# Four small moves in a one-core encoder-block kernel: an early fold, a late transform, an earlier load and a longer slow start

## The chip, the cores and the metric

The kernel runs on one core of a Trainium2 chip. A core has a matrix engine (TensorE, PE in the profile), two elementwise engines (VectorE, DVE; GpSimd, POOL), an engine for functions of one input (ScalarE, ACT) and a queue that issues transfers (SyncE, SP). Each engine runs its own instructions strictly in the order in which the program lists them, and waits for the others through semaphores. The metric is the device time of one execution in microseconds (us). Lower is better.

## The reference

Two batches of 2048 rows by 1024 columns (called s = 0 and s = 1 below) go through the same layer with the same weights. For every batch:

```
u  = rmsnorm(h)
z  = u @ w_in                 # columns: q 512 | k 128 | v 128 | ga 512 | f 512 | gf 512
q, k = rope(rmsnorm per head) # 8 q heads, 2 kv heads, head size 64
a  = softmax(q k^T / 8) v  * silu(ga)
fo = Re(2-D DFT of f over (positions, 64 channels)), times a 64x64 map for each of 8 groups, * silu(gf)
h  = h + [a, fo] @ w_out
y  = rmsnorm(h + (p @ w_ple) * sigmoid(rmsnorm(h) @ w_ple_gate))
```

All of it is float32 in and out. The kernel splits float32 numbers into a high and a low float16 part, and forms a product as three float16 products (high by high, high by low, low by high).

## The kernel before, in words

**Two long stages.** The first stage (`project`, L607) makes u and all products with w_in, row by row. The second stage runs attention (`attention`, L1252) and weaves into it a second stream of work, the *fill*: the rest of the Fourier branch and the output products of the block. Both stages are one instruction order that the program writes out by hand; no planner moves instructions later.

**The first stage** treats the 32 tiles of 128 rows in 16 pairs, eight pairs for each batch. For a pair i there is:

- `sq_u`, `newton`, `hi_u`, `lo_u`: the row norm, u split into two float16 halves (`hl`), and a transposing transfer on SP's queue that makes `uc`, the operand that TensorE needs.
- `mm_tile`: the q and kv products of each of the two tiles, and their copies out of PSUM (`z`, `vs`). `norm_q`, `rope_q`, `hi_q`, `lo_q` make q and k from them, on GpSimd, VectorE and ScalarE.
- *The fold.* Pairs other than a batch's first hold rows t and 2048-t. Their sum and difference go through the f weights in one product in place of two. `fold_u` (L810, GpSimd) adds the halves of u, `fold_s` (L816, GpSimd) forms sum and difference, `fold_hl` (L822) splits them again: high part on ScalarE (L827), low part on VectorE (L828). The result is `uf`. It is done in two halves, h = 0 and 1, each for half of the inner dimension. The buffer of `fold_s` (tag `sq`, one buffer) is shared with the squares of `sq_u` and of q and k.
- *The sweep* of the pair (`sweep_chunk`): the f product (48 narrow matmuls, L1039), a copy `ft` by ScalarE (L1007), the gf product of tile 0, then `first()` (L1009): one float32 product of `ft` with a 128x128 DFT matrix (two at L1012 in the profile; for a batch's first pair ten shorter ones at L1016 and L1027), a copy `ge` by ScalarE and a store `gd` issued by GpSimd; then the gf product of tile 1, and four ga products.

The sweep of a pair runs one iteration after its `mm_tile`, and is cut into steps: 57 for an ordinary pair, 65 for a batch's first (a step of f or gf is estimated in the program at 0.64 us, one of ga at 0.32). `sweep_part(us)` (L793) issues steps until that many estimated microseconds are spent; between such calls the iteration places the other work, so that this order is the order on every engine. Every fifth step (`NBF = 5`) calls one step of a background list: `weights_far` (loads, scales and stores the weights of the second stage), `embed_rows` (the same for p) and last `channel_map` (L540), which loads the cosine table, the 64x64 maps and two masks, waits a number of background steps, makes two block products (L556) and stores them for the second stage. Another fifth step, from pair 14's iteration on, calls one step of `ahead`: four empty steps and then the row maxima of the first 14 attention steps (`maxima`, L1319), each two matmuls into two banks (L1330), and one step later two reductions by VectorE (L1338).

**Banks and slots.** The eight PSUM banks are given out by a counter: of eight in turn five are `ps_x`, two `ps_g`, one `ps_f` (L195). Within a kind, the bank that was released first is taken first. The outputs of ScalarE in the sweep and the tiles of the background list share ten SBUF slots (tag `w2k`).

**The prologue.** Pairs 0 to 4 are started by an order of their own, since weights arrive and have to be split first. The fold of pair 1 stands in it (diff below): half 0 ahead of the work on pair 3 (`sq_u(3)`, `mid`, `make_u(3, 0)`, which contains the newton steps and `norm_q(0)`), half 1 behind it.

**The second stage** has 64 units of 8 attention steps. After each step the program lets the fill run for a budget (`interleave`, L1802). The fill is taken as 756 us of TensorE work; a step has a share of it: 0 for every fourth step (which carries the product with v), otherwise 0.85 up to step `FIRST` = 30, 1 up to step 255 and 1.15 after it (L1459). What the fill has left when attention is done runs behind it alone.

Of the kernel before, what the change touches and what calls it, by code (L numbers as in the profile page):

```python
# [33 lines left out]
NBF = 5  # L34
# [1 line left out]
AH = 2  # L36
FP = 2
RATE = 1.15
FIRST, SLOW = 30, 0.85
LAG = 3  # L40
P32 = 7
WHOLE = 2 * NT - 2
# [123 lines left out]
class Build:  # L166
# [373 lines left out]
    def channel_map(self, pool):  # L540

        nc, a = self.nc, self.a
        tl = lambda n, *s: pool.tile(list(s), F32, name=n, tag="w2k", bufs=self.nw2k)
        m12, wf = tl("m12", 64, 4, 128), tl("wfm", 64, 8, 64)
        bd = [tl("bd", 128, 512) for _ in range(2)]
        nc.sync.dma_start(m12[:], a["c_m12"])
        nc.sync.dma_start(wf[:], a["w_fmix"].rearrange("o g c d -> c (o g) d"))
        for v in range(2):
            nc.sync.dma_start(bd[v][:], a["c_mask"][v])
        for _ in range(4):  # L550
            yield
        for v in range(2):
            ps = self.bank()
            cut = 256 if v else 384
            for i, sl in enumerate((slice(0, cut), slice(cut, 512))):
                nc.tensor.matmul(ps[:, sl], m12[:, 2 * v + i, :], wf[:].rearrange("c g d -> c (g d)")[:, sl],  # L556
                                 start=True, stop=True)
            nc.vector.tensor_tensor(out=bd[v][:], in0=ps[:], in1=bd[v][:], op=ALU.mult)
            yield
            nc.sync.dma_start(self.bdd[:, v], bd[v][:])  # L560
# [46 lines left out]
    def project(self, P, PU, W, early, later, wkv, wq, wf, wgf, wga, bg, mid):  # L607
# [25 lines left out]
        def load_x(i, tt):  # L633
                s, c = steps[i]
                x = PU.tile([128, DM], F32, name="x", bufs=5)
                nc.sync.dma_start(x[:], self.xrow(s, c * CH + tt))
                X.setdefault(i, []).append(x)

        def sq_u(i):
            SU[i] = st.tile([128, CH], F32, name="n_su", bufs=3)  # L640
            for tt in range(CH):
                j = P.tile([128, 2 * DM], F16, name="jk", tag="sq", bufs=1)
                nc.scalar.activation(j[:, :DM], X[i][tt][:], AF.Square, accum_out=SU[i][:, tt:tt + 1])
# [149 lines left out]
        def sweep_part(us):  # L793

            while us > 0 and sweeps:
                try:
                    us -= next(sweeps[0])
                    if done:
                        done.append(True)
                        if len(done) % NBF == 0:  # L800
                            next(bg, None)
                        if len(done) % NBF == 2:
                            next(self.ahead, None)
                except StopIteration:
                    del sweeps[0]

        sweeps, done = [], []
        UF, FT, FS = {}, {}, {}

        def fold_u(i, h):  # L810

            FT[h] = P.tile([128, CH, 512], F32, name="f_t", tag="t2", bufs=1)
            x = lambda b: U[i][:, :, b, 4 * h:4 * h + 4, :].rearrange("p t k r -> p t (k r)")
            nc.gpsimd.tensor_tensor(out=FT[h][:], in0=x(0), in1=x(1), op=ALU.add)

        def fold_s(i, h):  # L816
            x = FT.pop(h)
            FS[h] = P.tile([128, 2, 512], F32, name="f_s", tag="sq", bufs=1)
            for y, op in enumerate((ALU.add, ALU.subtract)):
                nc.gpsimd.tensor_tensor(out=FS[h][:, y], in0=x[:, 0], in1=x[:, 1], op=op)  # L820

        def fold_hl(i, h):  # L822
            if h == 0:
                UF[i] = P.tile([128, 2, 2, 8, 128], F16, name="uf", bufs=1)
            o = lambda b: UF[i][:, :, b, 4 * h:4 * h + 4, :].rearrange("p y k r -> p y (k r)")
            x = FS.pop(h)
            nc.scalar.activation(o(0), x[:], AF.Copy)  # L827
            nc.vector.tensor_tensor(out=o(1), in0=x[:], in1=o(0), op=ALU.subtract)  # L828
# [6 lines left out]
        def make_u(i, iq=None):  # L835

            sq = square_z(iq) if iq is not None else None
            rs = newton(iq, i, sq)
            hi_u(i)
            for tt in range(CH):  # L840
                lo_u(i, tt)
            if iq is not None:
                norm_q(iq, rs)
# [5 lines left out]
        def iteration(i):  # L849
# [21 lines left out]
            if ok(i):  # L871
                sweep_part(4.0)
                VL.pop((i, 0))()
                sweep_part(4.0)
            if ok(i - 1):
                norm_q(i - 1, rs)
            if folds(i):
                fold_u(i, 0)
                fold_s(i, 0)
                fold_u(i, 1)  # L880
                sweep_part(8.0)
                fold_hl(i, 0)
                fold_s(i, 1)
                sweep_part(7.0)
                fold_hl(i, 1)
# [86 lines left out]
        del stores_next[:]  # L972
        fold_u(1, 0)
        fold_s(1, 0)
        sweep_part(5.8)
        fold_hl(1, 0)
        sq_u(3)
        sweep_part(5.8)
        mid()
        make_u(3, 0)  # L980
        fold_u(1, 1)
        load_x(5, 1)
        sq_u(4)
        fold_s(1, 1)
        sweep_part(6.0)
        fold_hl(1, 1)
        sweep_part(1000.0)
        append(1)
        done.append(True)
# [7 lines left out]
    def sweep_f(self, s, c, uc, UF, i, pool, W):  # L997

        nc = self.nc
        CH = 2  # L1000
        w2k = lambda n, k=512: pool.tile([128, 512], F32, name=n, tag="w2k", bufs=self.nw2k)
        F = []
        half = (slice(0, EVEN), slice(EVEN, 512))

        def out(ps):
            F.append(w2k("ft"))
            nc.scalar.activation(F[-1][:], ps[:], AF.Copy, scale=self.sc["inv_f"][:])  # L1007

        def first():  # L1009
            pf = self.bank()  # L1010
            if c:
                nc.tensor.matmul(pf[:], self.dft1[:], F[0][:], start=True, stop=True)  # L1012
            else:
                for y, sl in enumerate(half):
                    for t in range(CH):
                        nc.tensor.matmul(pf[64 * t:64 * t + 64, sl], self.dft1x[:, 2 * t + y], F[t][:, sl],  # L1016
                                         start=True, stop=True)
            ge = w2k("ge")
            nc.scalar.activation(ge[:], pf[:], AF.Copy)
            if c:  # L1020
                nc.gpsimd.dma_start(self.gd[s][:, c, :], ge[:])
                return 0.86
            for t in range(CH):
                nc.gpsimd.dma_start(self.gd[s].rearrange("(g y i) t d -> y g i t d", g=8, y=2)[t, :, :, 0, :],
                                    ge[64 * t:64 * t + 64])
            px, gx = self.bank(), w2k("ge")
            nc.tensor.matmul(px[0:64, :EVEN], self.dft1x[:, 4], F[0][:, :EVEN], start=True, stop=True)  # L1027
            nc.scalar.activation(gx[0:64, :EVEN], px[0:64, :EVEN], AF.Copy)
            nc.gpsimd.dma_start(self.gxd[s], gx[0:64, :EVEN])
            return 1.3  # L1030

        if c:
            ps = self.bank()
            uf = UF.pop(i)
            n = 0
            for k in range(8):
                for ia, ib in SPLIT3:
                    for y, sl in enumerate(half):
                        nc.tensor.matmul(ps[:, sl], uf[:, y, ia, k, :], W["f"][:, ib, k, sl], start=n == y == 0,  # L1039
                                         stop=n == 23, skip_group_check=True)  # L1040
                    n += 1
                yield 0.64
            out(ps)
        else:
            for tt in range(CH):
                ps = self.bank()
                yield from self.mm(ps[:], lambda b, k: uc[:, tt, b, k, :], lambda b, k: W["f"][:, b, k, :])
                out(ps)
        for tt in range(CH):
            t = c * CH + tt  # L1050
            ps = self.bank()
            yield from self.mm(ps[:], lambda b, k: uc[:, tt, b, k, :], lambda b, k: W["gf"][:, b, k, :])
            gt = w2k("gt")
            self.silu2(gt[:], ps[:], self.sc["h_gf"], w2k("th"),
                       lambda t=t, gt=gt: nc.gpsimd.dma_start(self.gfd[s][t], gt[:]))
            if tt == 0:
                yield first()

    def sweep_ga(self, s, c, uc, pool, W):

# [958 lines left out]
```

## Time and profile before

| | us |
|---|---|
| runs | 2654.62, 2664.98, 2664.23; median 2664.23 |
| the profiled execution | 2668.79 |
| its span, first to last instruction | 2667.0 |
| TensorE busy in it | 2530.7 (95%) |
| GpSimd busy | 1885.7 (71%) |
| VectorE busy | 1695.7 (64%) |
| ScalarE busy | 1186.3 (44%) |
| mean granted TensorE clock | 0.984 of full speed |

The span has three parts: the first stage to about 800 us, the second stage with attention to about 2600, and the rest of the fill to 2667. A line of the timeline gives the start, the duration, the engine, the line of the program, the operation, output<-inputs, the shape, the count and, in brackets, how long the engine stood before it and what it waited for. Lines of several instructions (x24) give the time from the first start to the last end. Matmul ends are modelled, so the 24 matmuls of a product overlap by a little with the next ones.

### The profile page before, as it was taken

The page shows a single profiled execution, that of the slowest core. Times are in us where ns is not written, and L with a number is a line of the kernel's source. Part 1 is how long each engine was busy: PE and PEld are TensorE (multiplying, and loading weights), DVE is VectorE, ACT ScalarE, POOL GpSimd, SP SyncE. Part 2 cuts the span into 40 slices and gives each one's busy share as a digit, 9 for nine tenths or more (in the row PEclk, how much of TensorE's full clock was granted, in tenths as well). Part 3 has the DMA queues.
Part 4 walks back from the last instruction along what each step waited for, and adds up shares of the span by engine and source line. Part 5 has one row for each costly group of instructions (what it writes and reads, how often), then busy time and mean ns, then how long its engine had stood idle before and what let it go on. Part 6 is the DMA issues. An engine that isn't in the chain of part 4 may idle for free. (4 is left out here: it accounts for less than half of the span.)

```text
span 2667.0 us, 49778 instructions
## 1 busy us (share of the span) xinstructions
PE 2530.7 (95%) x19896; PEld 1376.4 (52%) x19896; DVE 1695.7 (64%) x2318; ACT 1186.3 (44%) x1983; POOL 1885.7 (71%) x1570
## 2 busy tenths in 40 slices
PE   6699999998989999999999999999999999999998
PEld 3366665665655644544445454544444445544543
DVE  7676576886566766655666666656555666666634
ACT  4433354433225534444544444544445445544442
POOL 0365545454548878877888888888888888888870
PEclk9899999998999999999999999999999999999999
DMA  8357588765548733222222223323222222222223
GB/s 252 100 159 201 152 236 218 190 171 133 142 120 258 230 117 78 50 74 60 62 66 68 68 72 97 84 69 77 76 62 68 71 75 72 75 77 72 70 59 83
DMA packets 450601, 297.92 MB, mean 112 GB/s; under 512 B 294000, under 2 KB 394736, under 8 KB 450368
## 3 DMA queue, kind: packets, MB, share of 16 engines
q1 hardware_dynamic: 438512, 257.00, 37.5%
q0 software_dynamic: 11856, 37.74, 3.9%
q8 instruction: 155, 2.54, 0.4%
q14 instruction: 78, 0.64, 0.1%
HBM read 146.12 MB, written 82.45 MB: 86 GB/s over the span
## 5 line engine op out<-in xcount | busy, mean ns | idle before, releaser
L1308 POOL TENSOR_TENSOR acc<-acc,p 128x1024 f32<-128x1024 f32 x384 | 925.5, 2410 | 142.6 <-ACT p L1303 106.8
L1338 DVE TENSOR_REDUCE a_mx<-ps_m 128x1 f32<-128x1024 f32 x498 | 608.9, 1223 | 559.6 <-PE ps_m L1330 548.5
L1303 ACT ACTIVATE p<-ps_s,s_scale 128x512 f32<-128x512 f32 x1024 | 648.0, 684 | 669.4 <-PE ps_s L1300 637.2
L1627 PE MATMUL ps_g<-w_pg,hT 64*128 64x512 f16 x2784 | 497.4, 377 | 0.5 <-DVE h L1553 0.5
L1366 PE MATMUL ps_o<-p,v 128*64 128x256 f32 x4096 | 468.5, 382 | 0.0
L1300 PE MATMUL ps_s<-q,k 64*128 64x512 f16 x3072 | 436.6, 378 | 15.1 <-ACT p L1303 14.8
L1366 PEld LDWEIGHTS ps_o<-p,v 128*64 128x64 f32 x4096 | 283.9, 137 | 160.1 <-issue 28.5
L491 PEld LDWEIGHTS <-uc 128*128 128x128 f16 x2400 | 237.5, 99 | 240.4 <-issue 32.4
L1627 PEld LDWEIGHTS <-hT 64*128 64x128 f16 x2784 | 204.6, 94 | 156.5 <-issue 11.6
L1627 PE MATMUL ps_g<-w_wo,mh 64*128 64x512 f16 x1440 | 261.9, 378 | 15.3 <-DVE mh L1537 14.0
L1300 PEld LDWEIGHTS <-k 64*128 64x128 f16 x3072 | 152.0, 94 | 216.3 <-issue 95.6
L1627 PE MATMUL ps_g<-w_wo,mT 64*128 64x512 f16 x1440 | 259.9, 379 | 0.5 <-DMA mT<-mh 0.5
L1330 PE MATMUL ps_m<-k,q 64*128 64x512 f16 x996 | 201.8, 377 | 13.9 <-DVE a_mx L1338 13.9
L1306 POOL TENSOR_TENSOR acc<-p,p 128x1024 f32<-128x1024 f32 x64 | 150.9, 2358 | 28.2 <-ACT p L1303 27.4
L491 PEld LDWEIGHTS <-w_ga 128*128 128x128 f16 x1536 | 150.2, 99 | 30.0 <-DVE w_ga L373 3.7
L1627 PEld LDWEIGHTS <-mh 64*128 64x128 f16 x1440 | 101.0, 94 | 107.1 <-DVE mh L1537 19.2
L1627 PEld LDWEIGHTS <-mT 64*128 64x128 f16 x1440 | 103.9, 95 | 83.4 <-issue 6.4
L754 POOL TENSOR_TENSOR t<-t,t 128x1280 f32<-128x1280 f32 x16 | 46.3, 2891 | 123.3 <-DVE t L750 123.3
L491 PE MATMUL ps_x<-w_gf,uc 128*128 128x512 f16 x552 | 129.2, 391 | 0.8 <-DVE w_gf L373 0.4
L1074 POOL DMA_DIRECT2D agd<-gat x64 | 35.1, 549 | 118.7 <-DVE gat L1084 113.7
L491 PE MATMUL ps_x<-uc,w_ga 128*128 128x256 f16 x1008 | 117.2, 277 | 0.0
L1389 DVE RECIPROCAL ps_f<-ps_f 128x256 f32<-128x256 f32 x61 | 107.1, 1756 | 9.1 <-PE ps_f L1382 9.1
(338 smaller groups left out, 3413.3 us busy)
## 6 DMA issues: line engine op xcount, KB each, us to landing
q<-qTd SPq DMA_DIRECT2D x256, 64.0 KB, 2.2
ag<-agd SPq DMA_DIRECT2D x64, 256.0 KB, 3.3
out<-h POOLq DMA_DIRECT2D x31, 512.0 KB, 3.0
x<-in_x_prompt SPq DMA_DIRECT2D x16, 512.0 KB, 5.0
gfd<-gt POOLq DMA_DIRECT2D x32, 256.0 KB, 2.7
w_st<-in_w_out SPq DMA_DIRECT2D x32, 256.0 KB, 3.9
agd<-gat POOLq DMA_DIRECT2D x64, 128.0 KB, 2.7
w_st<-in_w_ple_gate SPq DMA_DIRECT2D x32, 256.0 KB, 4.3
```

The costliest lines, as they stand in the source:

```text
L491: self.nc.tensor.matmul(ps, lhs(ia, k), rhs(ib, k), start=(i == 0), stop=(i == 3 * ks - 1))
L754: nc.gpsimd.tensor_tensor(out=t1[:], in0=t1[:], in1=t2[:], op=ALU.add)
L1074: nc.gpsimd.dma_start(self.agd[s][1, r * 128:(r + 1) * 128, c * n:(c + 1) * n], gt[:, :n])
L1300: nc.tensor.matmul(S[u][e][:], w[sl], q[sl].rearrange("p h q -> p (h q)"), start=j == i == 0, stop=i + 1 == len(todo), skip_group_check=True)
L1303: nc.scalar.activation(p[:, e, :], S[u][e][:], AF.Exp, scale=self.sc["s_scale"][:])
L1306: nc.gpsimd.tensor_tensor(out=ACC[u][:], in0=P[u, 0][:], in1=p[:], op=ALU.add)
L1308: nc.gpsimd.tensor_tensor(out=ACC[u][:], in0=ACC[u][:], in1=p[:], op=ALU.add)
L1330: nc.tensor.matmul(ps[c], Q[u][0][sl, h, :], kt[s, kv, half][sl, :, 0, :], start=True, stop=True)
L1338: nc.vector.reduce_max(MX[u][:, h, half, c:c + 1], x, axis=AX.X)
L1366: nc.tensor.matmul(o[64 * f:64 * f + 64], vt[s, kv, c // 8][:, c % 8, :], p[:, e, f], start=(c == 0), stop=(c == 15))
L1389: nc.vector.reciprocal(r, r)
L1627: nc.tensor.matmul(g[0][:], g[1](ia, k)[sl], g[2](ib, k)[sl], start=a, stop=z, skip_group_check=True)
```

## The change

Five edits in one diff.

1. Both halves of the fold of pair 1 are placed ahead of `sq_u(3)`; the estimated 5.8 us of sweep between half 0 and `mid` are split 3.0 + 2.8, and the 6.0 that stood between the parts of half 1 goes into what follows.
2. `first()` stands behind both gf products, in every sweep.
3. `channel_map` waits 8 background steps between its loads and its products, in place of 4.
4. `ahead` is called in every fourth sweep step, in place of every fifth.
5. The small share of fill (0.85) holds for attention steps 0 to 60, in place of 0 to 30.

```
-FIRST, SLOW = 30, 0.85
+FIRST, SLOW = 60, 0.85
...
-        for _ in range(4):
+        for _ in range(8):
             yield
...
                         if len(done) % NBF == 0:
                             next(bg, None)
-                        if len(done) % NBF == 2:
+                        if len(done) % (NBF - 1) == 2:
                             next(self.ahead, None)
...
         fold_u(1, 0)
         fold_s(1, 0)
+        fold_u(1, 1)
         sweep_part(5.8)
         fold_hl(1, 0)
+        fold_s(1, 1)
+        sweep_part(3.0)
+        fold_hl(1, 1)
         sq_u(3)
-        sweep_part(5.8)
+        sweep_part(2.8)
         mid()
         make_u(3, 0)
-        fold_u(1, 1)
         load_x(5, 1)
         sq_u(4)
-        fold_s(1, 1)
-        sweep_part(6.0)
-        fold_hl(1, 1)
         sweep_part(1000.0)
...
             self.silu2(gt[:], ps[:], self.sc["h_gf"], w2k("th"),
                        lambda t=t, gt=gt: nc.gpsimd.dma_start(self.gfd[s][t], gt[:]))
-            if tt == 0:
-                yield first()
+        yield first()
```

More of the change, by code (lines that the diff above doesn't have):

```diff
@@ L38 @@
 RATE = 1.15
-FIRST, SLOW = 30, 0.85
+FIRST, SLOW = 60, 0.85
 LAG = 3
@@ L549, in channel_map @@
             nc.sync.dma_start(bd[v][:], a["c_mask"][v])
-        for _ in range(4):
+        for _ in range(8):
             yield
@@ L801, in sweep_part @@
                             next(bg, None)
-                        if len(done) % NBF == 2:
+                        if len(done) % (NBF - 1) == 2:
                             next(self.ahead, None)
@@ L974, in project @@
         fold_s(1, 0)
+        fold_u(1, 1)
         sweep_part(5.8)
         fold_hl(1, 0)
+        fold_s(1, 1)
+        sweep_part(3.0)
+        fold_hl(1, 1)
         sq_u(3)
-        sweep_part(5.8)
+        sweep_part(2.8)
         mid()
         make_u(3, 0)
-        fold_u(1, 1)
         load_x(5, 1)
         sq_u(4)
-        fold_s(1, 1)
-        sweep_part(6.0)
-        fold_hl(1, 1)
         sweep_part(1000.0)
@@ L1055, in sweep_f @@
                        lambda t=t, gt=gt: nc.gpsimd.dma_start(self.gfd[s][t], gt[:]))
-            if tt == 0:
-                yield first()
+        yield first()
     def sweep_ga(self, s, c, uc, pool, W):
```

## Prediction

> **What bounds the kernel now.** I read the page first, then the waits of TensorE up to 900 us, then the timeline of each engine around each wait.
>
> ```profile
> PE 2530.7 (95%) x19896; PEld 1376.4 (52%) x19896; DVE 1695.7 (64%) x2318; ACT 1186.3 (44%) x1983; POOL 1885.7 (71%) x1570
> ```
>
> ```profile
> PE ps_g L1039 <- ACT uf L827: 16.4, 1, 16.4
> PE ps_x L556 <- DMA wfm<-in_w_fmix: 7.4, 1, 7.4
> PE ps_f L1012 <- ACT ft L1007: 7.3, 2, 5.8
> PE ps_x L1330 <- DVE a_mx L1338: 4.6, 1, 4.6
> PE ps_g L1012 <- ACT ft L1007: 3.4, 1, 3.4
> PE ps_x L1012 <- DVE a_mx L1338: 2.6, 1, 2.6
> PE ps_x L1012 <- ACT ft L1007: 1.9, 1, 1.9
> ```
>
> TensorE is busy 95% of the span, so time is won only where it stands. These rows (total, times, longest) are stalls in the first stage that the edits touch: 43.6 us together. A stall costs more than its length, because the clock is lower behind it:
>
> ```profile
> 392.70 5.34 PE L491 MATMUL ps_g<-w_gf,uc 128*128 128x512 f16 x24
> 403.81 2.07 PE L1012 MATMUL ps_f<-ft,dft 128*128 128x512 f32 x2 [5.76 <-ACT ft L1007]
> 405.68 7.14 PE L491 MATMUL ps_x<-w_gf,uc 128*128 128x512 f16 x24
> 543.58 2.08 PE L1012 MATMUL ps_g<-ft,dft 128*128 128x512 f32 x2 [3.37 <-ACT ft L1007]
> 545.45 7.22 PE L491 MATMUL ps_g<-w_gf,uc 128*128 128x512 f16 x24
> 138.72 1.02 PE L1012 MATMUL ps_f<-ft,dft 128*128 128x512 f32 x2
> ```
>
> The same 24 matmuls take 5.34 and 7.14 us, the same two 1.02 and 2.07. So the stall of 5.76 costs 5.76 + 1.05 + 1.80 = 8.6, that of 3.37 costs 3.37 + 1.06 + 1.88 = 6.3.
>
> *By the skill:* the Trainium skill, "TensorE: Matmul & The Clock Gate", section on the HAM clock gate, says that an idle window of about 3.4 us halves the clock until about 3.4 us of activity; by that a long stall costs 1.7 us extra, and my sum would be some 5 us smaller, 2631. The rows show 2.8 to 2.9, and a slow stretch after 2.58 us too (below), so the rows decide.
>
> **Edit 1, the fold.**
>
> ```profile
> 106.94 2.78 PE L491 MATMUL ps_x<-wr_kv,uc 128*128 128x256 f16 x24
> 128.72 1.03 PE L1039 MATMUL ps_g<-w_f,uf 128*128 128x264 f16 x4 [16.38 <-ACT uf L827]
> 144.76 1.47 PE L491 MATMUL ps_x<-uc,w_ga 128*128 128x256 f16 x12
> 97.61 2.49 POOL L820 TENSOR_TENSOR f_s<-f_t 128x512 f32<-128x512 f32 x2
> 122.91 2.11 POOL L814 TENSOR_TENSOR f_t<-uc 128x1024 f32<-128x1024 f16 x1
> 102.47 1.06 ACT L643 ACTIVATE jk<-x 128x1024 f16<-128x1024 f32 x1 [1.29 <-DVE uf L828]
> 115.22 2.19 ACT L681 ACTIVATE hl<-x,rsq_z 128x1024 f16<-128x1024 f32 x2 [8.68 <-DVE rsq_z L284]
> 101.22 1.23 DVE L828 TENSOR_TENSOR uf<-f_s,uf 128x1024 f16<-128x1024 f32 x1 [6.64 <-ACT uf L827]
> 110.85 1.48 DVE L655 TENSOR_REDUCE q_ss<-sq 128x20 f32<-128x1280 f32 x1
> 116.40 5.96 DVE L690 SCALAR_TENSOR_TENSOR hl<-x,rsq_z,hl 128x1024 f16<-128x1024 f32 x2 [0.81 <-ACT hl L681]
> 151.62 2.16 DVE L828 TENSOR_TENSOR uf<-f_s,uf 128x1024 f16<-128x1024 f32 x1 [5.26 <-ACT uf L827]
> 159.27 1.22 DVE L828 TENSOR_TENSOR uf<-f_s,uf 128x1024 f16<-128x1024 f32 x1
> ```
>
> The rows are of TensorE, GpSimd, ScalarE and VectorE. Half 1 is late because GpSimd does `norm_q(0)` first and comes to its `fold_u` at 122.9. New order on GpSimd: `fold_s` half 0 to 100.1, `fold_u` half 1 (2.1) to 102.2; the low split of half 0 on VectorE, beside it, I give the 2.16 of the row at 151.62 rather than its 1.23, so that it ends at 103.4, which frees the one buffer; `fold_s` half 1 to 105.9; high split (1.06) 107.0; low split (1.23) 108.2. The f product wants it at 109.6. **The 16.4 us wait goes.** Behind these on GpSimd stand the stores gfd, gd and gxd and the rope tables, which nobody awaits here.
>
> But what was moved past now comes later. `sq_u(3)` needs the shared buffer: 108.2 instead of 102.5, to 110.6 (two squares of 1.06 and their sums). Behind it on ScalarE stands the tanh of the second gf product, then on VectorE its product: two passes over 512 columns, which I put at 0.7 each, 112.0. Its bank is, by the counter and the order of release, the one that the kv product (106.94) takes, and in the new order `first()` no longer lies between. So **kv waits from 107 to about 112**, a new stall of 5 us; with a slow clock behind it f ends near 122 and the first gf product near 127. The second gf product takes the `ps_f` bank of the first ga product, whose reader on VectorE is queued behind newton and `lo_u(3)`: the setup constants and newton run 6 us later than before (q_ss at 116.8 for 110.85), `hi_u(3)` at 121.2 for 115.22, `lo_u(3)` (5.96) ends at 128.4, the reader at 128.8. From there 5.2 + 0.9 us (gf, `first()`) bring ga to 134.9; it was 144.76. Gain **10 us**. Bounds: 18.5 if neither bank holds it (16.4 and 2.1 of slow clock), 6 if VectorE's queue is 4 us later. Later folds don't gain with it, their slack covers it: `uf` of pair 2 was whole at 160.5 (last row) for a product at 170.8 (next fence), and is now just in time for one at 161. The transposes behind `lo_u(3)` land near 134 by the 5 us that two of them take on SP's queue; their q product stands near 153 (134.9 + 10.5 of ga + 7.8 of q and kv).
>
> **Edit 2, the transform.** Only its place moves: two matmuls, one copy, one store on GpSimd's queue, all behind the second gate's. TensorE then reads `ft` 10.4 us behind the f product, not 5.2. Is ScalarE merely late, or too slow?
>
> ```profile
> 401.68 0.28 ACT L720 ACTIVATE vs<-ps_x 128x128 f32<-128x128 f32 x1 [6.85 <-DMA vd<-vs]
> 339.86 2.18 ACT L681 ACTIVATE hl<-x,rsq_z 128x1024 f16<-128x1024 f32 x2
> 261.36 0.69 ACT L1007 ACTIVATE ft<-ps_x,inv_f 128x512 f32<-128x512 f32 x1 [4.80 <-PE ps_x L1039]
> 386.11 2.17 ACT L681 ACTIVATE hl<-x,rsq_z 128x1024 f16<-128x1024 f32 x2
> 170.84 5.40 PE L1039 MATMUL ps_x<-w_f,uf 128*128 128x264 f16 x48
> 213.38 5.40 PE L1039 MATMUL ps_g<-w_f,uf 128*128 128x264 f16 x48
> ```
>
> Here too slow: between 300 and 440, with the background weights, ScalarE needs 46.2 us for a pair, TensorE unstalled 42.5. In that stretch TensorE is freed once, by the 5.2 us of extra room, however many waits are named; about 4 us of the third wait return. The wait at 543 is an isolated one, and its lag (a gf product of 5.2 and 3.37) fits into 10.4: that 6.3 goes whole. Gain 5.2 + 6.3, **11 us**; bounds 5 and 18.4 (1.5 + 1.9 + 8.6 + 6.3). `ft` holds one of ten slots 5 us longer; I take that as nothing while ScalarE has idle time (44% busy), and price its failure as a rival. The copy `ge` and its store are read in the second stage only.
>
> **Edit 3, the channel map.**
>
> ```profile
> 651.38 2.04 PE L556 MATMUL ps_x<-wfm,m 64*128 64x384 f32 x4 [7.41 <-DMA wfm<-in_w_fmix]
> 653.36 3.38 PE L491 MATMUL ps_x<-uc,w_ga 128*128 128x256 f16 x15
> 658.67 4.35 PE L491 MATMUL ps_x<-uc,w_ga 128*128 128x256 f16 x24
> ```
>
> The loads stay, the products move by 20 sweep steps, across a q/kv block, some 30 us on: the transfer has landed. 24 such matmuls take 2.78 when warm, so 1.6 us of slow clock lie in the third row, as much in the second, and 1 each in the two block products: 7.4 + 5.3, **12.7 us**. The two VectorE products and stores fall in pair 13's f and gf, some 100 us ahead of their reader in the second stage. Four slots are held longer, when the background list is done with them. Bounds 9 (some of the slow stretch stays) and 12.7.
>
> **Edit 4, maxima sooner.** Counting steps: products at steps 710, 718, ... 814 rather than 717, 727, ... 847; the last pair's sweep begins at 808, so one of 14 falls into it instead of four.
>
> ```profile
> 773.61 1.15 PE L1012 MATMUL ps_x<-ft,dft 128*128 128x512 f32 x2 [2.58 <-DVE a_mx L1338]
> 774.55 3.78 PE L491 MATMUL ps_x<-w_gf,uc 128*128 128x512 f16 x9
> 782.97 1.18 PE L1330 MATMUL ps_x<-k,q 64*128 64x512 f16 x2 [4.63 <-DVE a_mx L1338]
> ```
>
> Both waits with their slow stretches cost 12: 2.6, 1.8 (9 matmuls in 3.78, 2.0 warm), 4.6, 0.8, and 2 behind the last row. Reductions 13 and 14 will sit where these two sit in VectorE's queue, behind newton and `lo_q`. By the order of release the second gf product then needs a bank of the one (from 770.5 to 773.5), the first ga product of the other (from 779.5 to 783.0): 6.5 us of waits stay, but none is queued behind them. More calls in pairs 13 and 14 meet a VectorE that waits there; the memset, the scaling of maxima and the transposed load `mr` move forward with them. Gain **5**; bounds 0 and 12.
>
> **Edit 5, the slow start.** 756 us over 420.85 shares are 1.8 us a share; steps 31 to 60 hold 22 with a share, so 22 x 0.15 x 1.8 = 6 us of fill leave a stretch near 910 to 1010 us (3.5 us a step from 801) and run behind attention.
>
> ```profile
> 925.00:950.00 25.00, 22.11 (x168) 13.44 (x164) 20.41 (x25) 15.06 (x26) 24.78 (x16) 1.00 0.56 165
> 2600.00:2667.00 67.00, 57.02 (x265) 25.64 (x262) 30.08 (x82) 14.13 (x21) 3.13 (x6) 0.96 0.35 84
> ```
>
> The columns are busy us of PE, PEld, DVE, ACT, POOL. TensorE is near its bound there and in the tail up to the last output, so the work only changes places: gain **0**; bounds a loss of 6 (GpSimd at 24.78 of 25 sets the step, nothing is saved) and a gain of 5 (less VectorE load takes its waits away).
>
> **Sum.** 10 + 11 + 12.7 + 5 + 0 = 38.7, against the profiled 2668.79 (span 2667.0): 2630. The median of the runs lies 4.6 below that execution, so **2626**. All low bounds: 14 won, 2650; all high ones 67, 2598.
>
> **The rivals.**
>
> *A, every stall goes* (18.5 + 18.4 + 12.7 + 12 = 61.6): 2603. For it: ScalarE is only 44% busy. Against: the two bank waits and the 46.2 us period. 0.14.
>
> *B, the lead is given back.* If the 46.2 us period between 300 and 440 is set by SP's queue regardless of when TensorE comes, the prologue's 10 us end in a longer wait there; left are 11 + 12.7 + 5, 2636, or 2641 with 6 from edit 2. Against: ScalarE waited for TensorE at 261 (its `ft`, 4.80), so it was level then and follows a TensorE that comes sooner. 0.17.
>
> *C, the change doesn't do what it says:* the waits of edits 1 and 2 return in full as bank waits, only edit 3 stays, edit 5 costs 6: 2657, no change. 0.10.
>
> *D, slower: slots.* `ft` and the map's tiles starve the ten slots; ScalarE then waits for stores (the 6.85 above is such a wait, on another buffer). From 3.5 us a pair over the 11 pairs with background work it eats the 39; at the 5.2 for which `ft` is held it is 57, and 2682. For it: a lag of 11 is already there (392.70 to 403.81). Against: stalls only bite once the lag passes 10.4. 0.06.
>
> **How the numbers follow.** The forecast has 0.53. Half a percent is 13 us, about what a measurement of this kernel tells from no change; faster means below 2651: 0.51 of the forecast's, all of A, 0.16 of B and 0.03 of C, 0.84. Same 0.11, slower 0.05. The range 2604 to 2653 holds nearly all between the forecast's bounds, and B; it leaves out half of A, most of C, and D, 0.2.
>
> **What would show it.** Right: no wait for `uf` near 112, a new one of some 5 us at the kv product near 107, ga of pair 1 near 135; waits for `ft` only near 400, below 5 us; none for `wfm`; one or two for a_mx near the end of the stage, 3 us each; attention some 39 us earlier than 800.8, and a tail 6 us longer. Wrong: attention less than 25 us earlier (B, C), ScalarE waits for slots in every pair (D), or a second stage that is longer by more than 6 us.

## The result and the profile after

The changed kernel takes 2619.08 us (median of 4 runs, 2618.91 to 2622.64) against 2664.61 (2654.62 to 2671.83) for the kernel before on the same chip: a ratio of **0.9835, 95% interval 0.9802 to 0.9868**. The forecast of 2626 lies 7 us above that and the range held it. The way to it was another than forecast, though: some 23 us were won ahead of attention, where 39 were forecast, and 22.8 behind it, where none were.

The profiled execution took 2622.64 us, its span is 2620.9. In the lines of the changed kernel all line numbers beyond some L1055 are one lower than before (L1338 is now L1337). The busy line of its page, then, from the list of what TensorE waited for from 0 to 800 us, the rows that bear on the edits (columns: total, times, longest):

```profile
PE 2519.7 (96%) x19896; PEld 1387.2 (53%) x19896; DVE 1704.0 (65%) x2318; ACT 1184.5 (45%) x1983; POOL 1875.5 (72%) x1570
```

```profile
PE ps_x L1329 <- DVE a_mx L1337: 7.9, 1, 7.9
PE ps_x L491 <- DVE a_mx L1337: 5.8, 2, 3.3
PE ps_g L1012 <- ACT ft L1007: 4.6, 1, 4.6
PE ps_x L1012 <- ACT ft L1007: 3.9, 1, 3.9
PE ps_x L491 <- DVE gt L1083: 3.8, 1, 3.8
PE ps_f L491 <- DVE gat L1083: 2.2, 1, 2.2
```

The waits for `uf` (16.4) and `wfm` (7.4) are gone. Two bank waits stand in the place of the first, as forecast; two `ft` waits stay where one was forecast; and the longest of these, 7.9, is a wait that the forecast did not have. The same things in TensorE's timeline of the changed kernel, and behind it three rows of the kernel before (the first q product, f of pair 13, attention's first matmul):

```profile
32.35 0.59 PE L491 MATMUL ps_x<-wr_q,uc 128*128 128x512 f16 x1 [7.62 <-ACT wr_q L372]
109.40 4.45 PE L491 MATMUL ps_x<-wr_kv,uc 128*128 128x256 f16 x24 [3.83 <-DVE gt L1083]
126.51 7.03 PE L491 MATMUL ps_f<-w_gf,uc 128*128 128x512 f16 x24 [2.24 <-DVE gat L1083]
134.23 2.02 PE L491 MATMUL ps_x<-uc,w_ga 128*128 128x256 f16 x17
160.31 5.40 PE L1039 MATMUL ps_x<-w_f,uf 128*128 128x264 f16 x48
392.64 1.97 PE L1012 MATMUL ps_x<-ft,dft 128*128 128x512 f32 x2 [3.87 <-ACT ft L1007]
532.65 2.03 PE L1012 MATMUL ps_g<-ft,dft 128*128 128x512 f32 x2 [4.63 <-ACT ft L1007]
646.45 4.75 PE L1039 MATMUL ps_f<-w_f,uf 128*128 128x264 f16 x42
655.54 1.13 PE L556 MATMUL ps_x<-wfm,m 64*128 64x256 f32 x4
674.02 0.58 PE L1329 MATMUL ps_x<-k,q 64*128 64x512 f16 x1 [7.87 <-DVE a_mx L1337]
756.14 5.34 PE L491 MATMUL ps_x<-w_gf,uc 128*128 128x512 f16 x24 [2.50 <-DVE a_mx L1337]
765.60 6.68 PE L491 MATMUL ps_x<-uc,w_ga 128*128 128x256 f16 x48 [3.27 <-DVE a_mx L1337]
777.68 0.81 PE L1299 MATMUL ps_s<-q,k 64*128 64x512 f16 x6
```

```profile
34.00 0.58 PE L491 MATMUL ps_x<-wr_q,uc 128*128 128x512 f16 x1 [7.69 <-ACT wr_q L372]
678.45 1.80 PE L1039 MATMUL ps_x<-w_f,uf 128*128 128x264 f16 x15
801.00 0.81 PE L1300 MATMUL ps_s<-q,k 64*128 64x512 f16 x6
```

Attention begins 23.3 us earlier. To see where, cut the first stage at three rows: the first q product of the prologue (32.35 after, 34.00 before: 1.65 us of the 23.3 are there ahead of the change), f of pair 2 (160.31 and 170.84) and f of pair 13 (646.45 and 678.45). The stretches took 128.0 us against 136.8, 486.1 against 507.6, and 131.2 against 122.5. So 30.3 us were won, and **8.7 lost again** in the last stretch. Of both, 2.1 us are work that crossed a mark: the two block products of the channel map (1.06 us each at full clock) stand ahead of f of pair 13 in the kernel before (651.38 and 656.67) and behind its start in the changed one (651.13 and 655.54). Without them 28.2 us were won and 6.6 lost.

Why TensorE stood 7.87 us at 674 is on the other engines. The changed kernel's timelines of SP's queue, GpSimd and VectorE:

```profile
644.12 3.07 SPq L1269 DMA_DIRECT2D k<-kTd  x4
654.14 1.06 SPq L1275 DMA_DIRECT2D v<-vd  x2
655.24 0.43 SPq L625 DMA_DIRECT2D rt<-in_c_rope  x1
```

```profile
658.84 0.72 POOL L630 TENSOR_TENSOR rt<-rt,g_q_t 128x256 f32<-128x256 f32 x1 [8.78 <-DMA rt<-in_c_rope]
673.12 0.13 POOL L1333 MEMSET a_mx<- 128x16 f32 x1
```

```profile
673.28 1.29 DVE L1337 TENSOR_REDUCE a_mx<-ps_x 128x1 f32<-128x512 f32 x2 [8.16 <-POOL a_mx L1333]
```

VectorE's first reduction for the products made ahead waits for a memset of 0.13 us on GpSimd. That memset stands behind a norm and folds, the norm behind the small load `rt`, and SP issued `rt` only after 16 loads of k and q and two of v (644 to 655). The products, now ahead of time, meet a GpSimd that is late.

The second stage: what TensorE waited for from 800 us on, before and then after. (`p` is ScalarE's exponential of the scores; `mh` is the split input of the fill's output product, whose low half VectorE writes; `seen` is a copy of one column by which a bank is let go.)

```profile
PE ps_s L1300 <- ACT p L1303: 16.8, 42, 1.7
PE ps_g L1627 <- DVE mh L1537: 14.0, 10, 3.2
PE ps_m L1330 <- DVE a_mx L1338: 13.9, 18, 2.6
```

```profile
PE ps_m L1329 <- DVE a_mx L1337: 14.4, 20, 2.6
PE ps_g L1626 <- DVE seen L1592: 6.5, 2, 5.3
PE ps_s L1299 <- ACT p L1302: 3.6, 9, 0.9
PE ps_g L1626 <- DVE mh L1536: 1.7, 2, 1.0
```

And busy times from attention's first matmul to ScalarE's last `p`, then from there to the end, before and then after. The columns are the window and its length, busy us (and instructions) of PE, PEld, DVE, ACT and POOL, the granted clock, the share of the DMA engines and GB/s:

```profile
801.00:2580.00 1779.00, 1727.75 (x14810) 877.03 (x14808) 1098.98 (x1057) 862.36 (x1428) 1495.31 (x1205) 1.00 0.32 86
2580.00:2667.00 87.00, 77.02 (x396) 34.66 (x392) 36.16 (x89) 20.01 (x31) 15.21 (x30) 0.97 0.30 72
```

```profile
778.00:2513.00 1735.00, 1706.99 (x14748) 883.48 (x14744) 1096.97 (x1052) 862.17 (x1427) 1483.44 (x1205) 1.00 0.33 88
2513.00:2621.00 108.00, 92.54 (x458) 39.41 (x453) 43.97 (x95) 20.58 (x31) 17.69 (x30) 0.88 0.27 70
```

Attention is 44 us shorter: TensorE idles 28 us in it instead of 51, and is busy 20.8 us less, with 62 matmuls moved behind it. The rest of the fill is 21 us longer, with 15.5 more of busy time (at a lower clock) and 5.5 more of idle time. Net, 23 us.

### The profile page after: what moved, and what is told of

Same layout as the page of the kernel before. It is cut to its first block, busy times and chain, and to the rows that moved or that the text cites. A ratio compares the mean times of both kernels' runs of the same rounds, so it can differ in the third digit from the quotient of the medians.

```text
span 2620.9 us, 49788 instructions
## 1 busy us (share of the span) xinstructions
PE 2519.7 (96%) x19896; PEld 1387.2 (53%) x19896; DVE 1704.0 (65%) x2318; ACT 1184.5 (45%) x1983; POOL 1875.5 (72%) x1570
## 5 line engine op out<-in xcount | busy, mean ns | idle before, releaser
L1337 DVE TENSOR_REDUCE a_mx<-ps_m 128x1 f32<-128x1024 f32 x498 | 608.9, 1223 | 513.1 <-PE ps_m L1329 502.0
L491 PEld LDWEIGHTS <-w_ga 128*128 128x128 f16 x1536 | 152.0, 100 | 49.1 <-issue 22.8
L491 PE MATMUL ps_x<-w_gf,uc 128*128 128x512 f16 x480 | 106.0, 379 | 2.5 <-DVE a_mx L1337 2.5
## 6 DMA issues: line engine op xcount, KB each, us to landing
agd<-gat POOLq DMA_DIRECT2D x64, 128.0 KB, 2.8
```

The source lines that it names most:

```text
L491: self.nc.tensor.matmul(ps, lhs(ia, k), rhs(ib, k), start=(i == 0), stop=(i == 3 * ks - 1))
L1337: nc.vector.reduce_max(MX[u][:, h, half, c:c + 1], x, axis=AX.X)
```

## The experiments

All times stand against the kernel before, measured beside each; it had medians of 2661.4 to 2664.9 in all of them. The three stretches are those above. Equal code differs in them from run to run: over all runs of this section, 126.3 to 129.1 us in the first, 485.2 to 488.4 in the second, and in the last 128.2 to 131.6 in the five whose order there is the changed kernel's. In the rows "before" and "map 4 steps" the 2.1 us of the map's products belong to the second stretch, in the others to the last. Of the parts undone alone, only the slow start differs from the changed kernel beyond the intervals of the whole times; the prices of the others rest on the stretches.

| kernel | q to f(2) | f(2) to f(13) | f(13) to attention | time, us | ratio to before, 95% |
|---|---|---|---|---|---|
| before | 136.8 | 507.6 | 122.5 | 2664.61 | |
| after | 128.0 | 486.1 | 131.2 | 2619.08 | 0.9802 to 0.9868 |
| after, old fold | 136.9 | 485.2 | 131.2 | 2630.77 | 0.9861 to 0.9891 |
| after, old place of f's transform | 129.7 | 489.7 | 124.3 | 2622.96 | 0.983 to 0.9863 |
| after, map 4 steps | 128.4 | 500.8 | 123.2 | 2628.66 | 0.9848 to 0.9904 |
| after, ahead every 5th | 126.6 | 485.3 | 127.7 | 2616.75 | 0.9808 to 0.984 |
| after, memset on VectorE | 129.1 | 485.8 | 122.4 | 2614.35 | 0.98 to 0.9833 |
| the same, ahead every 5th | 126.4 | 485.6 | 127.2 | 2614.52 | 0.9808 to 0.984 |

### The longer slow start, undone alone and done alone

In the changed kernel:

```
-FIRST, SLOW = 60, 0.85
+FIRST, SLOW = 30, 0.85
```

and in the kernel before:

```
-FIRST, SLOW = 30, 0.85
+FIRST, SLOW = 60, 0.85
```

> The changed kernel with the small share of fill for 30 steps again (the last part of the change undone alone). Attention's first matmul stands at 777 us either way. Theory S, the longer small share is what made the stretch from attention's first matmul to the end 22.8 us shorter (1866.2 before, 1843.5 after): the stretch is 1866 again and the time some 2641 us. Rival T, that stretch is shorter because attention starts from another state (earlier, with other work left over), whatever the share: the stretch stays at 1843 and the time at 2619. In between if both share in it.

> The kernel before with the small share for 60 steps, nothing else changed. Attention starts at 801 us as before. Theory S: the stretch behind it falls from 1866 to about 1843, time 2642 us. Rival T: no change, 2664 us; and below 2664 by 6 at most if only the fill that moves counts.

Measured: 2642.87 us (0.9906 to 0.9938) and 2636.05 us (0.9889 to 0.9921). From attention's first matmul to the end it is 1866.0 us in the first (777.3 to 2643.3) and 1843.2 in the second (797.8 to 2641.0). Theory S holds: the last part of the change, alone, takes 22.8 us off that stretch, from whichever start (1866.0 before, 1843.2 after). The runs below that differ from the changed kernel only ahead of attention took 1839 to 1845 us there, so the difference is well clear of the spread. In the changed kernel with 30 steps, TensorE's waits for `p` and `mh` behind 800 us are near those of the kernel before again:

```profile
PE ps_s L1299 <- ACT p L1302: 15.7, 39, 1.7
PE ps_g L1626 <- DVE mh L1536: 9.7, 8, 2.4
```

### How much is held back, or when

Two kernels, one with

```
-FIRST, SLOW = 60, 0.85
+FIRST, SLOW = 30, 0.70
```

and one with

```
-FIRST, SLOW = 60, 0.85
+FIRST, SLOW = 90, 0.85
```

> The changed kernel with the slow start shortened to 30 steps again but at share 0.70 instead of 0.85: by step 60 the same share of fill is held back (22 x 0.30 = 6.6 against 44 x 0.15 = 6.6), only sooner. Theory P, what counts is how far the fill stands behind attention afterwards (its place against attention's units): the time stays at 2619 us, with p and mh waits of some 4 and 2 us behind 800 us. Theory Q, what counts is the lighter load in steps 31 to 60 themselves: the time goes back to 2641 us, with p and mh waits of some 16 and 10 us.

> The changed kernel with the small share for 90 steps, so 3.3 shares (6 us of fill) more held back. If the gain grows with what is held back: another 10 to 24 us less, 2595 to 2610 us. If 60 steps already took nearly all of the p and mh waits (5.3 us are left) and the rest only swells the work behind attention: 2614 to 2625 us. If it is a matter of where the fill's tiles happen to fall against attention's units: some of the waits come back, 2625 to 2645 us.

Measured: 2624.5 us (0.9838 to 0.9868) and 2628.17 us (0.985 to 0.9884). The third, run last, has the memset of the next experiment as well:

```
-                    nc.gpsimd.memset(MX[u][:], -3e38)
+                    nc.vector.memset(MX[u][:], -3e38)
-FIRST, SLOW = 60, 0.85
+FIRST, SLOW = 45, 0.85
```

> The changed kernel with the memset on VectorE and the small share for 45 steps, half way between 30 and 60. So far, from attention's first matmul to the last p and from there to the end of the span: 1778.5 and 87.5 us with 30 steps, 1735.4 and 108 with 60, 1731 and 113 with 90. If both follow what is held back evenly: 1757 and 98 us, with attention's start at 771 a time of 2626 us, worse than the 2614 of 60 steps. If the waits for p and mh go at some point short of 45 and the rest only swells the tail: 1735 to 1743 and 95 to 101 us, a time of 2603 to 2613 us, better than both kernels.

Measured: 2620.86 us (0.9834 to 0.9867). Side by side, from attention's first matmul to the start of the last row of `p`, and from there to the end, of each kernel. Held back: the steps up to and with number `FIRST` that carry a share, 24, 35, 46 or 69 by the program's rule, times 1 less the share; the expectations counted a little fewer.

| slow start | shares held back | attention | rest | both |
|---|---|---|---|---|
| 30 steps at 0.85 | 3.6 | 1779 | 87 | 1866 |
| 45 at 0.85 | 5.3 | 1760 | 90 | 1851 |
| 60 at 0.85 | 6.9 | 1735 | 108 | 1843 |
| 30 at 0.70 | 7.2 | 1743 | 102 | 1845 |
| 90 at 0.85 | 10.4 | 1731 | 113 | 1844 |

Theory P holds in its main point: about the same amount held back sooner gives the same stretch within the spread, so the load of steps 31 to 60 is not what matters. (Of its waits, mh came to 0.9 us and p to 7.1, more than the 4 expected.) In the profiles the gain grows with the amount to some 7 shares and stops there: at 10.4 attention loses another 4 us, and the rest gains 5. The whole times say less for 90 steps: the profiled execution (2622.61) was the fastest of its four, and the median of 2628.17 lies in the range expected if waits come back. In that profile they did not: `p` has 3.8 us, `mh` none, and new are 3.4 us for `acc_h` and 2.4 more for `h`. Whether 90 steps are worse than 60 stays open, since the intervals overlap. The expectation for 45 steps, "both follow evenly" at 1757 and 98, is nearer than its rival, though the rest grew by only 3. What it is in attention that a later fill spares, wait by wait, no run took apart.

### The memset

```
-                    nc.gpsimd.memset(MX[u][:], -3e38)
+                    nc.vector.memset(MX[u][:], -3e38)
```

> The changed kernel with one edit: the memset that prepares a_mx for the products made ahead is issued on VectorE instead of GpSimd. Theory: the 7.87 us wait at 674 us is the first reduction's wait for that memset, which stands in GpSimd's order behind a norm that waits for a late load; the memset on VectorE takes it away, attention starts 11 to 14 us earlier (763 to 766 us) and the time is 2605 to 2608 us. Rival, VectorE itself is late there or the products meet another wait at the same place: the stall stays at 5 us or more and the time at 2617 to 2620 us.

Measured: 2614.35 us (0.98 to 0.9833). The wait of 7.87 us is gone; the longest at these products is now 1.89 us, at a later one of them:

```profile
676.95 0.37 PE L1329 MATMUL ps_x<-k,q 64*128 64x512 f16 x1 [1.89 <-DVE a_mx L1337]
```

The last stretch falls from 131.2 to 122.4 us, 8.8 where 11 to 14 was expected, and attention starts at 771.2, not by 766 (the run was 1.6 us later at the first q product). The cause is shown; the price was set too high. It is known only roughly: the last stretch took 128.2 to 131.6 us in five runs with the memset on GpSimd and 122.1 to 122.4 in three with it on VectorE, which is 5.8 to 9.5 us. In whole times the gain over the changed kernel, 4.7 us between medians taken on different occasions, is within their intervals.

### The ahead products, with the stall and without

```
-                        if len(done) % (NBF - 1) == 2:
+                        if len(done) % NBF == 2:
```

> The changed kernel with the ahead products asked for at every 5th step again. Theory: the 7.87 us wait for a_mx at 674 us and the slow clock behind it (some 11 to 14 us together) go, and the waits near the end of the first stage come back at their size of before (6 us more): attention starts at about 770 us and the time is 2609 to 2614 us. Rival, the part is worth the 5 us that the forecast gave it and the stall at 674 us comes with any spacing: attention starts at 783 us, time 2624 us.

> The changed kernel with the memset on VectorE and the ahead products at every 5th step again. It measures the fourth part alone, free of the stall at 674 us, against the kernel with the memset on VectorE and every 4th step (attention's first matmul 122.4 us after f of pair 13 begins). The forecast's price: 5 us dearer, 127 us. Rival, the part is worth nothing because the waits near the end of the stage only change places: 122 to 123 us. In time 2609 to 2619 us.

Measured: 2616.75 us (0.9808 to 0.984) and, with the memset moved, 2614.52 us (0.9808 to 0.984). With the memset on VectorE, every 4th step against every 5th is 122.4 against 127.2 us in the last stretch: the part alone is worth **4.8 us** there, against the 5 of the forecast; the whole times of the two, 2614.35 and 2614.52, do not tell them apart. One of the waits of the kernel before stands there again, longer than its 4.63:

```profile
753.09 0.58 PE L1329 MATMUL ps_x<-k,q 64*128 64x512 f16 x1 [6.38 <-DVE a_mx L1337]
```

With the memset on GpSimd it is 128.2 to 131.6 against 127.7: the stall is the price of sooner products and eats up at least what they win. The stall at 674 does not come "with any spacing", but the theory's 770 us for attention's start was missed too (772.6), and so was its time of 2609 to 2614.

### The fold

The hunk of the prologue goes back: half 1 of the fold behind `make_u(3, 0)`, as in the kernel before.

> The changed kernel with the second pair's folds back in their old order (first part of the change undone alone). Theory: the wait of 16.4 us for uf comes back in place of those of 3.8 and 2.2 us, and the lead that it costs stays lost: attention's first matmul at 786 to 788 us instead of 777.7 and the time 2627 to 2630 us. Rival, the period of 46.2 us between 300 and 440 us takes the lead back whenever it was won: attention starts at 777 to 780 us with smaller ft waits, time 2619 to 2622 us.

Measured: 2630.77 us (0.9861 to 0.9891), attention at 786.99. The wait is back, and of the lead that it costs nothing returns later (the other stretches are equal within 1 us):

```profile
128.44 1.03 PE L1039 MATMUL ps_g<-w_f,uf 128*128 128x264 f16 x4 [16.46 <-ACT uf L827]
```

### f's transform

```
+            if tt == 0:
+                yield first()
-        yield first()
```

> The changed kernel with f's transform behind the first gate product again (second part undone alone). Theory: the ft waits at 393 and 533 us grow to the 5.8 and 3.4 us of before and one more returns, with slow clocks 7 us in all by the traces (the forecast said 11): attention's first matmul at 784 to 789 us, time 2626 to 2631 us. Rival, once the prologue runs ahead ScalarE has caught up and the place of the transform no longer matters: 777 to 779 us, time 2619 us.

Measured: 2622.96 us (0.983 to 0.9863), attention at 778.71. Neither was quite right. With the fold placed early TensorE comes sooner, and the waits for `ft` are more than in the kernel before (9.88 in the prologue is new):

```profile
131.02 2.07 PE L1012 MATMUL ps_f<-ft,dft 128*128 128x512 f32 x2 [9.88 <-ACT ft L1007]
534.05 2.08 PE L1012 MATMUL ps_g<-ft,dft 128*128 128x512 f32 x2 [3.56 <-ACT ft L1007]
679.93 0.37 PE L1330 MATMUL ps_x<-k,q 64*128 64x512 f16 x1 [3.10 <-DVE a_mx L1338]
```

By f of pair 13, 5.3 us are lost (1.7 and 3.6); the 1.7 lie within the spread of equal code there, the 3.6 little beyond it. Then the last row: a TensorE that comes later waits 3.10 us at the late memset and not 7.87, and 6.9 us return. From the first q product to attention the kernel without the part is even 1.6 us shorter (743.7 against 745.3), and the intervals of the whole times overlap: what the part is worth in the changed kernel as a whole is not shown. Ahead of that stall a lead is partly lost whatever won it.

### The channel map

```
-        for _ in range(8):
+        for _ in range(4):
             yield
```

> The changed kernel with the channel map's products after 4 steps of the background list again (third part undone alone). Theory: TensorE then asks for the map 14.8 us sooner after the lead of the other parts, so the transfer is as late as before or later: a wait of 7 to 12 us for it with slow clock behind, attention's first matmul at 785 to 793 us instead of 777.7, less whatever the stall for a_mx shortens by because GpSimd catches up meanwhile (up to 8). Rival, that stall takes all of it back: attention at 778 us and the time at 2619 us.

Measured: 2628.66 us (0.9848 to 0.9904), attention at 786.16.

```profile
PE ps_x L556 <- DVE tmax L1071: 9.0, 1, 9.0
PE ps_x L1329 <- DVE a_mx L1337: 4.4, 1, 4.4
```

The wait of 9.0 us is back. The list puts it to a short reduction that came last, but the load of `wfm` was issued at 634.4, took 3.5 us to land, and the product starts at 638.0. By f of pair 13 it is 14.7 us, of which 2.1 are the two products themselves, which stand ahead of that mark here: the part is worth 12.6. The last stretch is 8.0 us shorter, 2.1 of it for the same reason; the other 5.9 come back at the stall at the memset, now 4.4: the same pattern as with `ft`.

### The copy that holds the last shared bank

```
-                nc.vector.tensor_copy(j[:], low[0][:, 0:1])
+                nc.scalar.activation(j[:], low[0][:, 0:1], AF.Copy)
```

> The changed kernel with the memset on VectorE, and with the one-column copy that lets the last shared bank go (seen) on ScalarE instead of VectorE. In the changed kernel the copy stands on VectorE behind a product that waits for GpSimd and a reciprocal, and TensorE waits 5.35 us for it at 2535.85, then runs at a slow clock. Theory: ScalarE is through with what stands ahead of it at 2532.9, so 2.7 us of the wait go and some slow clock with it: 2609 to 2613 us against 2614 with the memset alone. Rival, another wait takes its place in the tail: 2614 us.

Measured: 2619.08 us (0.9824 to 0.9861). In the tail the rival was right: the wait for `seen` falls from 5.3 to 1.8, one for VectorE's `h` takes its place, and from the last `p` to the end it is 107.6 us against 108.1 with the memset alone:

```profile
PE ps_g L491 <- DVE h L1576: 5.8, 1, 5.8
PE ps_g L1626 <- ACT seen L1592: 2.9, 2, 1.8
```

That its span is 9.4 us longer, where the rival expected none, comes from attention. There a wait of 1.68 us for a_mx at 838 us with a slow clock behind it is new, which stands ahead of the first of the two moved copies (938.7 us); no run shows what brought it, nor the rest of the 9.4.

## Why the prediction was right, and where it was not

The time came out by luck, because two errors of opposite sign cancelled: 17 us too much ahead of attention (38.7 forecast; 30.3 less 8.7 came), 22.8 too little behind it. By its own test, "attention less than 25 us earlier" is wrong, and it was 23.3.

- **The fold: right.** No wait for `uf`; bank waits at the kv product of 109 (3.83; some 5 forecast) and at the second gf product (2.24, to 126.5; 128.8 forecast); ga of pair 1 at 134.2 (134.9 forecast). The first q product had come 1.65 us earlier, which the change did not do; with that added the two are 128.2 and 135.9. Price 8.9 us by the experiment, 10 forecast.
- **f's transform: sized too high.** 11 us forecast, 5.3 measured by f of pair 13, with the spread said above. The step that failed is, of the wait at 543, "that 6.3 goes whole": a wait of 4.63 us stands there still, at 533. The forecast let `ft` keep its lag behind f (8.6 us) while TensorE reads it later. But f of that pair began 17.4 us earlier than before (512.26 for 529.63) and `ft` only 10.9 (531.93 for 542.86), since ScalarE stands ahead of it for a store of `vs` and then for VectorE's `p_f`, as it did in the kernel before (5.93 and 5.73 us). The wait of 3.87 at 393 was forecast (near 400, about 4). The two waits of ScalarE in the changed kernel:

```profile
524.15 0.28 ACT L720 ACTIVATE vs<-ps_x 128x128 f32<-128x128 f32 x1 [5.99 <-DMA vd<-vs]
531.12 0.91 ACT L471 ACTIVATE p_hl<-p_in,p_f 128x256 f16<-128x256 f32 x2 [6.69 <-DVE p_f L466]
```

- **The channel map: right.** No wait, full clock; 12.6 us, 12.7 forecast.
- **The ahead products: the forecast's own price held (4.8 against 5), one step failed.** It let "the memset [...] move forward with them" at no cost. It had to be asked where the memset stands on GpSimd and what GpSimd waits for at that time: the load `rt`, behind k, q and v in SP's queue. With that, the stretch behind f of pair 13 is 8.8 us longer than with the memset on VectorE (5.8 to 9.5 over the runs). The two waits near the end came as forecast: 2.50 and 3.27, up to 756 and 766 us.
- **The slow start: wrong.** The step was "TensorE is near its bound there [...] so the work only changes places". It was read from one window of 25 us and from the rest of the fill. TensorE's idle time in attention was 51 us, 30.8 of it in 42 waits for `p` and 10 for `mh` behind 800 us, and 23 of it went. The forecast priced the work held back (6 us) and not these waits, 21.5 us of which stand between 1000 and 1600 us, mostly behind the stretch of steps 31 to 60. The tail, forecast 6 us longer, came 21 longer. Its bounds, a loss of 6 and a gain of 5, were a judgement on that one window.
- **The rivals.** "The lead is given back" came true in part, at another place: at the memset near 674 us, not between 300 and 440. ScalarE did follow the lead of the prologue, as argued against it: between 300 and 540 us every `ft` came 9.4 to 12.8 us sooner. It did not follow TensorE's further lead (17.4 us at 512). "Slots starve" did not come, and no part failed to do what it says.

With the sizes measured, the sum reads 8.9 + 5.3 + 12.6 + 4.8, less 8.8 for the stall, plus 22.8, which is 45.6; the spans differ by 46.1, of which 1.65 stood ahead of the change, so 44.4. The two lie closer together than the spread of equal code (up to 3.4 us in a stretch) lets one claim.

The fastest of the versions is the changed kernel with the memset on VectorE, 2614.35 us, level with the one that also asks at every 5th step; that it beats the changed kernel rests on the last stretch of the traces, since the intervals of the whole times overlap.

## What to carry to other kernels

When work moves forward, follow each instruction that moves with it to its place on its own engine, the cheapest ones too: a memset of 0.13 us behind a late load cost 6 to 9. Price a change of pacing by all waits of the stage that it paces, grouped over the whole stage, not by one window at its beginning. And measure parts by stretches between fixed rows, taking care that no moved work has crossed a row (here 2.1 us had): a stall late in a stage gives back what an earlier part lost, so that undoing a part that had won 5.3 us up to there changed attention's start by 1.

## What the runs showed that was not expected

After the wait of 5.35 us at 2535.85 in the changed kernel, TensorE's clock stayed at half long after it had work again. Its row, and windows of the same stretch with the columns as above (the clock is the number behind the five busy times):

```profile
2535.85 6.56 PE L1626 MATMUL ps_g<-w_pg,hT 64*128 64x512 f16 x15 [5.35 <-DVE seen L1592]
```

```profile
2537.00:2540.00 3.00, 3.00 (x8) 1.04 (x7) 0.00 (x0) 0.00 (x0) 0.00 (x0) 0.50 0.97 258
2549.00:2552.00 3.00, 3.00 (x9) 1.08 (x9) 0.03 (x1) 0.69 (x1) 0.00 (x0) 0.50 0.19 36
2552.00:2555.00 3.00, 3.00 (x12) 1.21 (x11) 1.45 (x2) 0.00 (x0) 0.00 (x0) 0.76 0.13 43
676.00:678.00 2.00, 2.00 (x12) 1.44 (x10) 1.50 (x3) 0.00 (x0) 1.98 (x3) 0.50 0.64 242
680.00:682.00 2.00, 2.00 (x21) 1.80 (x20) 1.68 (x4) 0.25 (x1) 0.56 (x1) 1.00 0.00 0
```

Behind the 7.87 us at 674.02 full speed is back by 680, behind this one only after 2552, 16 us on with TensorE busy throughout. The Trainium skill, "TensorE: Matmul & The Clock Gate", section on the HAM clock gate, has the full clock return after about 3.4 us of sustained activity: the stretch at 674 agrees roughly (0.50 to 678, 1.00 from 680), the one at 2536 does not, by a factor of about five. The granted clock of the rest of the fill, 0.97 before and 0.88 after, is where a part of what attention saved went. What held the clock there no run shows.
